# Weight sums, modulation rows, squares and the first w_mod of a two-layer denoising step: who does them, and when

## The chip, the cores and the metric

The kernel runs on one core of a Trainium2 chip. The metric is the device time of one execution in microseconds (us), from the profiler of the device; where several runs were made, their median.

## What is computed

A network of two layers works on 128 context tokens and 512 latent tokens, 640 in all (T), each 1024 numbers wide. In each layer, for the two groups of tokens:

```python
sh1, sc1, g1, sh2, sc2, g2 = split(silu(cond) @ w_mod + b_mod, 6)   # two conditions: context, latent
h = rmsnorm(x, norm1_g) * (1 + sc1) + sh1
z = h @ w_in                     # feeds an RG-LRU, two attentions and three branch gates
merged = sigmoid(ga) * (o_a @ w_oa) + sigmoid(gb) * (o_b @ w_ob) + sigmoid(gc) * (o_c @ w_oc)
x = x + g1 * (merged @ w_out)
h = rmsnorm(x, norm2_g) * (1 + sc2) + sh2
gate, val = split(h @ w_up, 2)   # 2 x 2816 columns
x = x + g2 * ((gelu(dwconv(gate)) * val) @ w_down)
```

After the layers a last RMSNorm gives the output. All is in 32-bit floating point.

## The kernel before

Tokens lie along the free dimension: an activation is eight tiles of 128 channels x 640 tokens. A matrix product in full precision is made of three (mm3): every operand is split into a high half (a rounded copy, made by ScalarE) and a low half (what is left, a subtraction on VectorE), and high x high, high x low and low x high are summed in PSUM. Tokens are worked in two halves of 320 columns.

**Order.** The program is a set of streams (generators): side (attention), lru, fill (modulation, `mod_stream`) and main. A clock that counts the estimated time of TensorE decides which stream goes on: a stream yields either a delay, or a mark of another stream (`("up", l)`, `("down", l, g)`, `("h", l, w, half)`) and a lag. TensorE's instructions stand in the order in which they are written. The other engines' instructions, and the DMA issues on SP, are put in order by a scheduler that goes by priority and by its own estimate of when an instruction is ready; `with self.soon(n)` makes instructions more urgent by n places, `MLOW = -200` less urgent. Each engine then works its list in order.

**Feed-forward part.** `ffn` makes the first three of 22 chunks of w_up directly (PLAIN). The other 19 are "pairs" (`pair`): a 2 x 2 block product done with seven smaller products instead of eight, in the order 1, 6, 7, 5, 4, 2, 3, each of 12 matmuls into one of six PSUM banks. `pair_weights` loads the four raw blocks of the next pair and makes their sums on GpSimd, in lines 1512 to 1515:

```python
e.tensor_tensor(out=s1, in0=a21, in1=a22, op=ALU.add)
e.tensor_tensor(out=a21, in0=a11, in1=a21, op=ALU.subtract)
e.tensor_tensor(out=s2, in0=s1, in1=a11, op=ALU.subtract)
e.tensor_tensor(out=s4, in0=a12, in1=s2, op=ALU.subtract)
```

`parts` makes the high (L1528) and low halves of a block after the current pair's product of the same number. For products 4, 2 and 3 (BY_DMA) the low half is made by ScalarE, which writes -x, and by a DMA with addition that GpSimd issues (L1531); for the others by VectorE (L1533). s1, s2 and s4 have one place each, used pair after pair. PSUM is read by VectorE (`add`, L1561). The gate's convolution is L1486 and L1488.

Chunks come in groups of 5, 4, 4, 4 and 5. After each group, `staggered` multiplies by the rows of w_down that belong to it (the down stage): eight output chunks, the first two together, each weight loaded and split by `wload` (L300 high, L303 low). `residual` scales by g2; in the first four groups (src is None) this is ScalarE's (L1363), and `done` adds the chunk to the tensor x_middle by a DMA with addition from GpSimd (L1691). In the last group, and in the output projection (`project`), `residual` also adds (VectorE, L1368), `square` sums the squares for the next RMSNorm (L608 on ScalarE, L610 on VectorE), and the last three chunks are worked half by half. After each half `norm_stream` forms the row sums of the squares on TensorE (`rstd`) and modulates the half (L657, L661, L662) with priority MSOON = 1500; the residual of these chunks has 3000.

**Modulation.** The vector of 6 x 1024 columns per layer is made in six parts v = 0 to 5 of eight blocks of 128 columns. `mods` makes parts by columns on TensorE: 32 matmuls of the condition (32 columns wide) with w_mod as the moving side into PSUM; the result is transposed. `mods_rows` makes one part on VectorE: for each block a load of 128 columns of the transposed w_mod (512 KB, tensor wmodt, L569), and two products with the condition that sum along the row (L578), with priority MLOW. The condition lies in four places of F (cond_rows, `get_cond`, L557). F is a pool of 22 places of 128 x 648 that all temporary tiles share; the place that has been free longest is given out.

In `mod_stream` layer 0's part 5 is made by columns after ("up", 0), layer 1's part 2 by rows after ("down", 0, 0) with a pace of 15, parts 0 and 1 by columns behind it, part 3 by rows after ("h", 1, 0, 1), part 4 by rows after the second attention, part 5 by columns after ("up", 1). At the very start parts 0 and 1 of layer 0 come from the tensor wmod in 32 loads of two runs of 1 KB a row (`start`, L1735).

Of the kernel before, what the change touches and what calls it, by code (L numbers as in the profile page):

```python
# [13 lines left out]
AF = mybir.ActivationFunctionType  # L14
ALU = mybir.AluOpType
AX = mybir.AxisListType

P = 128
D = 1024
KC = 8  # L20
SEQ = 128
LAT = 512
T = SEQ + LAT
# [5 lines left out]
FF_GROUPS = ((0, 5), (5, 4), (9, 4), (13, 4), (17, 5))  # L29
PLAIN = 3  # L30
# [142 lines left out]
class Net:  # L173
# [13 lines left out]
    MLOW, AFTER, PACE = -200, 8, (3.0, 2.0, 3.0, 15.0, 5.0)  # L187
# [6 lines left out]
    BY_DMA = (4, 2, 3)  # L194

# [287 lines left out]
    def mods(self, l, v, ahead=2, pace=0):  # L483

        n = 8 if v % 3 == 2 else 16
        yield from self.mods_columns(l, 8 * v, n, ahead, pace or self.PACE[1])
# [11 lines left out]
    def mods_columns(self, l, c0, n, ahead, pace):  # L498
# [16 lines left out]
        for k in range(KC):  # L515
            ws = q_.popleft()
            for j in range(4):
                o = j * w % 512
                self.matmul(
                    w / 2.2e3, out=acc[32 * j : 32 * j + 32, :w], lhsT=self.cond[:, k], rhs=ws[j * w // 512][:, o : o + w],  # L520
                    start=(k == 0), stop=(k == KC - 1), tile_position=(0, 32 * j),
                )
            self.F.put(*ws)
            if k + ahead < KC:
                q_.append(load(k + ahead))
            yield pace
# [830 lines left out]
    def residual(self, l, dst, src, b, m, half, gate):  # L1357
# [3 lines left out]
        for i, lo, hi in segs:  # L1361
            if src is None:
                self.nc.scalar.activation(  # L1363
                    out=dst[:, lo:hi], in_=b[:, lo - c0 : hi - c0], func=AF.Identity,
                    scale=self.mod[:, l, gate + m, i : i + 1],
                )
                continue
# [5 lines left out]
    def staggered(self, l, src, xs, gate, chunk, after, early, done=None, ahead=None, lead=None):  # L1373
# [20 lines left out]
        for m in range(n0, KC - late):  # L1394
            w = self.wload(src(m))
            x = chunk(m)
            for half in range(2):
# [24 lines left out]
        for half in range(2):  # L1422
            for w, x, m in zip(ws, cs, ms):
# [3 lines left out]
                if after is not None:  # L1427
                    self.square(x, m, half)
# [66 lines left out]
    @property  # L1495
    def sum_engine(self):
        return self.nc.gpsimd

    def pair_weights(self, l, j):


        nc, e = self.nc, self.sum_engine
# [11 lines left out]
        e.tensor_tensor(out=s2, in0=s1, in1=a11, op=ALU.subtract)  # L1514
        e.tensor_tensor(out=s4, in0=a12, in1=s2, op=ALU.subtract)
# [38 lines left out]
    def pair(self, l, j, ws, then, gv, during):  # L1554
# [44 lines left out]
        gv.append((xh, xl))  # L1599

# [6 lines left out]
    def ffn(self, l):  # L1607
# [28 lines left out]
        for g, (c0, nch) in enumerate(FF_GROUPS):  # L1636
# [60 lines left out]
            yield from self.staggered(l, src, gv, 40, chunk, after, early, done, ahead, lead)  # L1697
# [317 lines left out]
```

## Time and profile before

| | |
|---|---|
| median of 3 runs | 2439.75 us (2432.13 to 2444.91) |
| the profiled execution | 2437.27 us |
| its span, first to last instruction | 2435.5 us |
| TensorE busy | 2358.5 us, 97% |
| VectorE busy | 1721.6 us, 71% |
| ScalarE busy | 1189.1 us, 49% |
| GpSimd busy | 368.6 us, 15% |
| moved by DMA | 323.42 MB, 133 GB/s |

In the profile PE is TensorE, PEld its weight load, DVE VectorE, ACT ScalarE, POOL GpSimd, SP the queue that issues most DMAs. L578 is line 578 of the kernel. All times are of one execution; a matmul's end is modelled. PEclk is the granted clock of TensorE as a share of full speed (2.4 GHz).

### The profile page before, as it was taken

To read this page: it belongs to the slowest core of one execution; us is meant where nothing else is said; L and a number is where in the kernel's file an instruction comes from. 1 tells how busy PE (TensorE), PEld (TensorE's weight loads), DVE (VectorE), ACT (ScalarE), POOL (GpSimd) and SP (SyncE) were. 2 spreads that over 40 slices of the span, in tenths; PEclk is the share of its full clock that TensorE was granted. 3 is DMA by queue.
4 is the path that set the end of the run, shared out by engine and by line. 5 is a ranking of instruction groups with operands and counts; after the bars stand their busy time and mean duration, and the time that the engine had idled before them with its cause. 6 is when DMAs were issued, how large, how long until landed. Compare 5 with 4: busy or idle time off the path is not lost. (4 is left out here: it accounts for less than half of the span.)

```text
span 2435.5 us, 43194 instructions
## 1 busy us (share of the span) xinstructions
PE 2358.5 (97%) x16591; PEld 2254.8 (93%) x16591; DVE 1721.6 (71%) x3329; ACT 1189.1 (49%) x2413; POOL 368.6 (15%) x490
## 2 busy tenths in 40 slices
PE   8999999999999989999999999999999999999998
PEld 7899999998999888989999999999888989999998
DVE  6588878756767776655768688877667776755776
ACT  5237665723334445555543557565233354555553
POOL 0000000000000344444300000000000003543450
PEclk9999999999999999999999999999999999999999
DMA  8752222322552667685644322223226635656663
GB/s 289 236 180 72 91 71 82 98 66 72 158 177 85 187 160 177 169 209 118 173 158 146 100 91 79 82 71 97 64 76 203 207 118 125 152 126 148 136 147 115
DMA packets 162286, 323.42 MB, mean 133 GB/s; under 512 B 16272, under 2 KB 49568, under 8 KB 162080
## 3 DMA queue, kind: packets, MB, share of 16 engines
q1 hardware_dynamic: 140768, 277.66, 35.1%
q0 software_dynamic: 21312, 43.00, 11.1%
q8 instruction: 131, 2.15, 0.4%
q14 instruction: 75, 0.61, 0.1%
HBM read 244.29 MB, written 54.29 MB: 123 GB/s over the span
## 5 line engine op out<-in xcount | busy, mean ns | idle before, releaser
L277 PE MATMUL g<-r,wh 128*128 128x320 f32 (+1 forms) x5752 | 1304.7, 314 | 14.3 <-ACT f L1363 6.2
L277 PEld LDWEIGHTS g<-r,wh 128*128 128x128 f32 x5752 | 960.0, 189 | 43.3 <-issue 21.4
L277 PE MATMUL g<-r,wl 128*128 128x320 f32 (+1 forms) x2876 | 893.0, 311 | 13.8 <-DMA wl<-wr 4.8
L277 PEld LDWEIGHTS g<-r,wl 128*128 128x128 f32 x2876 | 544.3, 189 | 17.3 <-DMA wl<-wr 6.2
L303 DVE TENSOR_TENSOR wl<-wr,wh 128x1024 fp32r<-128x1024 f32 (+2 forms) x227 | 233.2, 1028 | 117.1 <-ACT wh L300 104.5
L277 PE MATMUL g<-r,k 128*128 128x320 f32 (+2 forms) x1256 | 216.4, 313 | 6.7 <-ACT f L1363 2.0
L277 PEld LDWEIGHTS g<-r,k 128*128 128x128 f32 x1256 | 192.4, 190 | 14.2 <-issue 3.3
L300 ACT CAST wh<-wr 128x512 fp32r<-128x512 f32 (+2 forms) x137 | 107.5, 785 | 168.9 <-PE g L277 98.7
L1470 POOL MEMSET f<- 128x1 f32 x132 | 31.9, 361 | 994.2 <-DMA f<-x_kept 226.8
L1001 DVE TENSOR_REDUCE sm<-s 128x1 f32<-128x640 f32 (+3 forms) x104 | 92.9, 893 | 89.1 <-PE s L277 88.6
L277 PE MATMUL g<-r 128*128 128x322 f32 (+2 forms) x628 | 124.1, 317 | 2.0 <-ACT f L1276 1.0
L1488 DVE SCALAR_TENSOR_TENSOR f<-f,vec 128x641 f32<-128x641 f32 x88 | 115.4, 1319 | 14.6 <-ACT f L1486 13.7
L277 PE MATMUL g<-wh,r 128*128 128x256 f32 x576 | 107.4, 282 | 0.0
L277 PEld LDWEIGHTS g<-r 128*128 128x128 f32 x628 | 100.5, 192 | 6.7 <-ACT f L1201 2.1
L578 DVE SCALAR_TENSOR_TENSOR s<-f 128x1024 f32<-128x1024 f32 x64 | 79.8, 1248 | 34.4 <-DMA f<-in_wmodt 28.9
L1528 ACT CAST wh<-f 128x512 fp32r<-128x512 f32 x116 | 71.0, 617 | 63.9 <-PE g L277 34.2
L277 PE MATMUL tb<-r,k 128*128 128x320 f32 x636 | 101.6, 309 | 0.3 <-DVE r L1586 0.3
L1363 ACT ACTIVATE f<-g,mod 128x192 f32<-128x192 f32 (+2 forms) x166 | 65.5, 436 | 70.5 <-PE g L277 55.5
L1533 DVE TENSOR_TENSOR wl<-f,wh 128x512 fp32r<-128x512 f32 x68 | 62.2, 920 | 51.8 <-ACT wh L1528 51.8
L1533 DVE TENSOR_TENSOR k<-f,k 128x512 fp32r<-128x512 f32 x78 | 63.8, 836 | 48.0 <-ACT k L1528 46.7
L1128 POOL MEMSET f<- 128x3 f32 (+1 forms) x48 | 4.3, 141 | 608.8 <-DMA q_kept<-f 151.3
L277 PEld LDWEIGHTS tb<-r,k 128*128 128x128 f32 x636 | 95.3, 188 | 0.5 <-DVE r L1586 0.5
(252 smaller groups left out, 4273.0 us busy)
## 6 DMA issues: line engine op xcount, KB each, us to landing
wr<-in_win SPq DMA_DIRECT2D x77, 512.0 KB, 3.4
f<-in_wmod SPq DMA_DIRECT2D x128, 256.0 KB, 4.5
wr<-in_wup SPq DMA_DIRECT2D x44, 512.0 KB, 4.7
f<-in_wup SPq DMA_DIRECT2D x40, 512.0 KB, 4.6
x_middle<-f POOLq DMA_DIRECT2D x64, 320.0 KB, 5.5
f<-in_wmodt SPq DMA_DIRECT2D x32, 512.0 KB, 4.7
wr<-in_wqkv SPq DMA_DIRECT2D x24, 512.0 KB, 4.0
wl<-f POOLq DMA_DIRECT2D x48, 256.0 KB, 5.2
```

The source lines that it names most:

```text
L277: self.nc.tensor.matmul(**kw)
L300: nc.scalar.copy(wh[:, :n], raw[:, :n])
L303: self.sub_engine().tensor_tensor(out=wl[:, o : o + c], in0=raw[:, o : o + c], in1=wh[:, o : o + c].bitcast(F32), op=ALU.subtract)
L578: nc.vector.scalar_tensor_tensor(out=junk, in0=w.ap, scalar=1.0, in1=self.cb[i].ap, op0=ALU.mult, op1=ALU.mult, accum_out=self.mod[:, l, j ...
L1001: nc.vector.tensor_reduce(out=m_[:, lo:hi], in_=src, axis=AX.XY if hi - lo == 1 else AX.X, op=ALU.max)
L1128: nc.gpsimd.memset(xp[:, c0:c1], 0.0)
L1363: self.nc.scalar.activation(out=dst[:, lo:hi], in_=b[:, lo - c0 : hi - c0], func=AF.Identity, scale=self.mod[:, l, gate + m, i : i + 1],)
L1470: nc.gpsimd.memset(gp[:, c : c + 1], 0.0)
L1488: nc.vector.scalar_tensor_tensor(out=g[:, :n], in0=gp[:, k : k + n], scalar=fw(k), in1=g[:, :n], op0=ALU.mult, op1=ALU.add)
L1528: self.nc.scalar.copy(h, x)
L1533: self.nc.vector.tensor_tensor(out=lo, in0=x, in1=h.bitcast(F32), op=ALU.subtract)
```

## The change

- `pair_weights`: the sums s2 and s4 are made by VectorE instead of GpSimd.
- `residual`, where it only scales: the second half is done by VectorE (tensor_scalar) instead of ScalarE.
- `staggered`, last chunks: `square` stands inside the same `soon(3000)` as the residual.
- `mod_stream`: layer 1's parts 0, 1 and 2 are all made by rows. Each step of `mods_rows` waits for the next mark of the list SLACK: the end of a pair that is not the last of its group, or the begin of output chunk 2, 3 or 4 of a down stage (29 marks, for 30 steps with 24 blocks). The condition is fetched once for the three. Parts 3 and 4 of layer 1 come one behind the other after ("h", 1, 0, 1), with a pace of 4.5 for 5.0.
- `mods_columns` does two of eight steps at a time (per = 2) with twice the pace, for part 5 of both layers.
- wmod is laid out in the order of its loads, one run of 2 KB a row.

The diff without its context lines:

```diff
@@ -187 +187 @@
-    MLOW, AFTER, PACE = -200, 8, (3.0, 2.0, 3.0, 15.0, 5.0)
+    MLOW, AFTER, PACE = -200, 8, (3.0, 2.0, 3.0, 0.0, 4.5)
@@ -195,0 +196,5 @@
+    SLACK = [
+        x for g, (c0, n) in enumerate(FF_GROUPS)
+        for x in [("pair", 0, j) for j in range(max(c0, PLAIN), c0 + n - 1)] + [("chunk", 0, g, m) for m in (2, 3, 4)]
+    ]
+
@@ -483 +488 @@
-    def mods(self, l, v, ahead=2, pace=0):
+    def mods(self, l, v, ahead=2, pace=0, per=1):
@@ -486 +491 @@
-        yield from self.mods_columns(l, 8 * v, n, ahead, pace or self.PACE[1])
+        yield from self.mods_columns(l, 8 * v, n, ahead, pace or self.PACE[1], per)
@@ -498 +503 @@
-    def mods_columns(self, l, c0, n, ahead, pace):
+    def mods_columns(self, l, c0, n, ahead, pace, per):
@@ -515,11 +520,12 @@
-        for k in range(KC):
-            ws = q_.popleft()
-            for j in range(4):
-                o = j * w % 512
-                self.matmul(
-                    w / 2.2e3, out=acc[32 * j : 32 * j + 32, :w], lhsT=self.cond[:, k], rhs=ws[j * w // 512][:, o : o + w],
-                    start=(k == 0), stop=(k == KC - 1), tile_position=(0, 32 * j),
-                )
-            self.F.put(*ws)
-            if k + ahead < KC:
-                q_.append(load(k + ahead))
+        for k0 in range(0, KC, per):
+            for k in range(k0, k0 + per):
+                ws = q_.popleft()
+                for j in range(4):
+                    o = j * w % 512
+                    self.matmul(
+                        w / 2.2e3, out=acc[32 * j : 32 * j + 32, :w], lhsT=self.cond[:, k], rhs=ws[j * w // 512][:, o : o + w],
+                        start=(k == 0), stop=(k == KC - 1), tile_position=(0, 32 * j),
+                    )
+                self.F.put(*ws)
+            for k in range(k0 + ahead, min(k0 + ahead + per, KC)):
+                q_.append(load(k))
@@ -1363,4 +1369,9 @@
-                self.nc.scalar.activation(
-                    out=dst[:, lo:hi], in_=b[:, lo - c0 : hi - c0], func=AF.Identity,
-                    scale=self.mod[:, l, gate + m, i : i + 1],
-                )
+                scale = self.mod[:, l, gate + m, i : i + 1]
+                if half:
+                    self.nc.vector.tensor_scalar(
+                        out=dst[:, lo:hi], in0=b[:, lo - c0 : hi - c0], scalar1=scale, scalar2=None, op0=ALU.mult
+                    )
+                else:
+                    self.nc.scalar.activation(
+                        out=dst[:, lo:hi], in_=b[:, lo - c0 : hi - c0], func=AF.Identity, scale=scale
+                    )
@@ -1373 +1384 @@
-    def staggered(self, l, src, xs, gate, chunk, after, early, done=None, ahead=None, lead=None):
+    def staggered(self, l, src, xs, gate, chunk, after, early, done=None, ahead=None, lead=None, name=None):
@@ -1396,0 +1408 @@
+            self.mark("chunk", l, name, m)
@@ -1427,2 +1439,2 @@
-                if after is not None:
-                    self.square(x, m, half)
+                    if after is not None:
+                        self.square(x, m, half)
@@ -1495,4 +1506,0 @@
-    @property
-    def sum_engine(self):
-        return self.nc.gpsimd
-
@@ -1502 +1510 @@
-        nc, e = self.nc, self.sum_engine
+        nc, e, v = self.nc, self.nc.gpsimd, self.nc.vector
@@ -1514,2 +1522,2 @@
-        e.tensor_tensor(out=s2, in0=s1, in1=a11, op=ALU.subtract)
-        e.tensor_tensor(out=s4, in0=a12, in1=s2, op=ALU.subtract)
+        v.tensor_tensor(out=s2, in0=s1, in1=a11, op=ALU.subtract)
+        v.tensor_tensor(out=s4, in0=a12, in1=s2, op=ALU.subtract)
@@ -1599,0 +1608 @@
+        self.mark("pair", l, j)
@@ -1697 +1706 @@
-            yield from self.staggered(l, src, gv, 40, chunk, after, early, done, ahead, lead)
+            yield from self.staggered(l, src, gv, 40, chunk, after, early, done, ahead, lead, g)
@@ -1727 +1735,0 @@
-        src = io["wmod"].rearrange("(r p) (g n c) -> n r p g c", p=P, g=2, n=n_)
@@ -1735 +1743 @@
-                nc.sync.dma_start(out=place.rearrange("p (g c) -> p g c", g=2)[:, :, :w], in_=src[n, r])
+                nc.sync.dma_start(out=place, in_=io["wmod"][n, r])
@@ -1883,2 +1891 @@
-        yield from self.mods(0, 5)
-        yield ("down", 0, 0), 0
+        yield from self.mods(0, 5, 2, 4.0, 2)
@@ -1886 +1893,4 @@
-        yield from self.mods_rows(1, 2, self.PACE[3], 1)
+        steps = deque(self.SLACK)
+        for v in range(3):
+            for x in self.mods_rows(1, v, 0, 1):
+                yield (steps.popleft(), self.PACE[3]) if steps else 0
@@ -1888,4 +1898,3 @@
-        yield from self.mods(1, 0, 2, 9.0)
-        for mark, v in ((("h", 1, 0, 1), 3), (("o", 1, 1), 4)):
-            yield mark, 0
-            self.get_cond()
+        yield ("h", 1, 0, 1), 0
+        self.get_cond()
+        for v in (3, 4):
@@ -1893,3 +1902,3 @@
-            self.F.put(*self.cb)
-        yield ("up", 1), 2
-        yield from self.mods(1, 5)
+        self.F.put(*self.cb)
+        yield ("up", 1), 0
+        yield from self.mods(1, 5, 2, 4.0, 2)
@@ -1910 +1919,3 @@
-    out = {"x": f(x.T.reshape(KC, P, T)), "wmod": f(i["w_mod"][0, :, : 2 * D])}
+    out = {"x": f(x.T.reshape(KC, P, T)), "wmod": i["w_mod"][0, :, : 2 * D]}
+
+    out["wmod"] = f(out["wmod"].reshape(KC, P, 2, 4, 256).transpose(3, 0, 1, 2, 4).reshape(4, KC, P, 512))
```

## Rows read from the trace of the kernel before

**Rows 1.** the page: busy us (share of the span) xinstructions
```profile
PE 2358.5 (97%) x16591; PEld 2254.8 (93%) x16591; DVE 1721.6 (71%) x3329; ACT 1189.1 (49%) x2413; POOL 368.6 (15%) x490
```

**Rows 2.** TensorE's waits, whole trace: us in total, times, longest us
```profile
PE g L277 <- ACT f L1363: 8.2, 8, 2.6
PE g L277 <- DVE wl L303: 6.7, 6, 3.6
PE pv L277 <- DMA wl<-wr: 6.5, 4, 2.5
PE pv L277 <- DVE f L610: 6.5, 2, 3.2
PE g L277 <- DMA wl<-wr: 4.8, 4, 1.9
PE g L277 <- DMA wl<-f: 4.1, 4, 1.7
```

**Rows 3.** windows after a wait: engines' busy us (xinstructions), then granted clock, DMA
```profile
756.70:763.60 6.90, 6.04 (x25) 6.05 (x26) 2.79 (x8) 0.17 (x1) 0.00 (x0) 0.51 0.22 76
```

**Rows 4.** windows: layer 0's and layer 1's feed-forward part
```profile
757.60:1244.30 486.70, 463.30 (x3084) 443.65 (x3084) 323.17 (x530) 246.40 (x484) 182.35 (x199) 0.98 0.64 164
1968.10:2424.60 456.50, 444.98 (x3018) 436.21 (x3018) 298.69 (x487) 241.26 (x475) 177.33 (x199) 0.99 0.56 133
```

**Rows 5.** timeline of VectorE, end of layer 0's output projection: start, us, engine, line
```profile
750.30 0.55 DVE L1368 SCALAR_TENSOR_TENSOR f<-g,mod,f 128x320 f32<-128x320 f32 x1 [0.19 <-PE g L277]
...
757.01 0.48 DVE L610 TENSOR_TENSOR f<-f 128x320 f32<-128x320 f32 x1
```

**Rows 6.** TensorE's groups by form: busy us, mean ns
```profile
L277 PE MATMUL s<-f,cond 128*32 128x512 f32 x128 | 17.0, 605 | 0.0
```

**Rows 7.** TensorE's waits between 1024 and 1056 us
```profile
PE g L277 <- ACT f L1363: 5.3, 4, 2.6
```

**Rows 8.** VectorE's groups by form: busy us, mean ns | idle before
```profile
L578 DVE SCALAR_TENSOR_TENSOR s<-f 128x1024 f32<-128x1024 f32 x64 | 79.8, 1248 | 34.4 <-DMA f<-in_wmodt 28.9 <-DMA f<-cond_rows 5.3
L1533 DVE TENSOR_TENSOR k<-f,k 128x512 fp32r<-128x512 f32 x78 | 63.8, 836 | 48.0 <-ACT k L1528 46.7 <-PE tb L277 1.2
...
L303 DVE TENSOR_TENSOR wl<-wr,wh 128x512 fp32r<-128x512 f32 x68 | 47.8, 702 | 65.8 <-ACT wh L300 65.2
...
L1368 DVE SCALAR_TENSOR_TENSOR f<-g,mod,f 128x320 f32<-128x320 f32 x24 | 13.1, 549 | 22.4 <-PE g L277 22.4
```

**Rows 9.** timeline of VectorE, layer 0's first down stage
```profile
853.47 1.23 DVE L578 SCALAR_TENSOR_TENSOR s<-f 128x1024 f32<-128x1024 f32 x1 [3.66 <-DMA f<-in_wmodt]
...
855.95 1.55 DVE L303 TENSOR_TENSOR wl<-wr,wh 128x640 fp32r<-128x640 f32 x2
```

**Rows 10.** windows at the begin of layer 1
```profile
1268.00:1318.50 50.50, 50.50 (x421) 50.50 (x420) 41.78 (x93) 15.08 (x31) 0.00 (x0) 1.00 0.48 157
1320.00:1360.00 40.00, 40.00 (x338) 40.00 (x338) 28.06 (x73) 11.38 (x28) 0.28 (x4) 1.00 0.50 155
```

**Rows 11.** TensorE's waits between 1795 and 1925 us
```profile
PE g L277 <- DVE r L1444: 2.6, 2, 1.4
```

**Rows 12.** GpSimd's groups by form: busy us, mean ns | idle before
```profile
L1514 POOL TENSOR_TENSOR f<-f 128x512 f32<-128x512 f32 x20 | 36.6, 1830 | 0.0
...
L1515 POOL TENSOR_TENSOR f<-f 128x512 f32<-128x512 f32 x20 | 27.7, 1384 | 73.1 <-DMA wl<-f 73.0
```

**Rows 13.** timeline of GpSimd, layer 0's second group
```profile
910.40 1.88 POOL L1514 TENSOR_TENSOR f<-f,wr 128x512 f32<-128x512 f32 x1
912.22 2.65 POOL L1531 DMA_DIRECT2D wl<-f  x3
```

**Rows 14.** timeline of TensorE at the same place
```profile
915.56 0.42 PE L277 MATMUL g<-r,wl 128*128 128x320 f32 x1 [1.69 <-DMA wl<-f]
```

**Rows 15.** window of the first loads of w_mod
```profile
12.70:19.90 7.20, 6.29 (x53) 5.39 (x53) 0.65 (x2) 0.88 (x3) 0.00 (x0) 0.73 1.08 388
```

**Rows 16.** GpSimd's waits, whole trace
```profile
POOL f L1515 <- DMA wl<-f: 104.7, 26, 5.2
```

## What I predict, and from what

> **What bounds the kernel now.** I read the page's busy times first. TensorE has work in 2358.5 us of a span of 2435.5 [rows 1], so 77 us of idle time are all that hiding something can win, besides work taken off TensorE itself. Then I read the list of what TensorE waits for [rows 2]: no wait is large. The reader is to see that four of its six rows belong to the feed-forward part (residuals on ScalarE, L1363; low weight halves that come by DMA, wl) and one, L610, to a single place in each layer. Next the windows after a wait [rows 3]: the granted clock is 0.51 of full, the lower level of 1.2 GHz, in a stretch that begins while TensorE stands still. The trace has three such stretches of 6.8 us after the first 23 us (from 756.7, 855.7 and 1968.4) and five of 3.4 us (from 900.1, 1186.8, 1261.9, 1866.0 and 1903.6). At half speed they lose 3.4 and 1.7 us each, about 19 us in all. A wait of 2 to 4 us can so cost twice its length. Last, the two feed-forward parts side by side [rows 4]: the same products take 486.7 us in layer 0 and 456.5 in layer 1, though TensorE's clock and instructions are alike. Layer 0's 30 us more are what the streams of modulation cost there: matmuls on TensorE, and waits.
>
> **The change part by part.** The sum is made against the profiled execution, 2437.3 us, which lies 2.5 below the median of the runs, 2439.75.
>
> *Squares first.* At the end of the output projection VectorE has the last residual done at 750.9, but the last sum of squares (L610) is run at 757.01, behind the first half's modulation, and TensorE waits until then for its row sums [rows 5]. That is 6.5 us in two waits [rows 2], each followed by a slow stretch of 6.8 us [rows 3], which costs 3.4. With the square as urgent as the residual (3000 against 1500 for modulation) it runs first and both go: 6.5 + 6.8 = 13.3. What it is put ahead of moves by one operation of 0.48 us, and TensorE reaches that half only after its 12 row sums. I take -13. At the end of layer 0 and of the kernel the same edit meets no wait of this size: 0.
>
> *Rows in place of columns for layer 1's first 16 columns.* Half of the 128 recorded matmuls in [rows 6] belong to mods(1, 0), and 17.0/2 = 8.5 us of TensorE work go: -8.5. Also gone are 32 loads of 256 KB on SP's queue; 16 of 512 KB come, the same bytes. The columns held eight places of F, the rows hold six (four for the condition, two for the load), but all through layer 0's feed-forward part. While the columns ran, residuals found no free place, since the last write to x_middle had not landed: 5.3 us of waits on L1363 [rows 7], of 8.2 in the whole trace [rows 2]. So some 3 us are spread over the other seven down stages. I leave 0.8 to this one: -4.5.
>
> *Where the row blocks stand.* One block is two products of 1.25 us [rows 8] on VectorE. Block 2 of layer 0's down stage shows the danger: the product stood 3.66 us before its load had landed, the low weights (L303) stood behind both products [rows 9], and TensorE waited 3.6 us, the longest wait on L303 [rows 2], and lost 3.4 more in the slow stretch from 855.7: -7 when these eight blocks are moved. But 24 blocks come, spread behind pairs and chunks. From one side they cost nothing: eight blocks ran between 1268 and 1318.5 with TensorE busy in 50.5 of 50.5 us [rows 10]. From the other, 7 us for those eight make 0.9 a block, 21 us. I take half, +11, since what decided was a load that came late, and the next load is still issued only one step ahead. Behind a chunk a step is short, so that end isn't excluded.
>
> *Modulation 4 moved from the second projection to behind modulation 3.* There VectorE's work delayed TensorE by 2.6 us on L1444 [rows 11] with two slow stretches of 3.4 (from 1866.0 and 1903.6): -2.6 - 3.4 = -6. In the new place VectorE is busy 28.06 of 40 us and TensorE without a gap [rows 10]: 0 there, at worst the 7 us of the eight blocks above.
>
> *Two of four weight sums to VectorE.* On GpSimd they are L1514 and L1515, 1.83 and 1.38 us [rows 12]. The low halves' DMAs are issued from the same queue: at 910.40 L1514 begins, at 912.22 the three DMAs follow [rows 13], TensorE waits for the first of them 1.69 us until 915.56 [rows 14]. Waits for such DMAs sum to 6.5 + 4.8 + 4.1 = 15.4 us in 12 [rows 2], 1.3 a wait, and two slow stretches (from 900.1 and 1186.8) add 3.4: 18.8. A DMA that is issued 1.8 us sooner closes most of them; one that stood behind L1512 or L1513, or before a landing that is late anyway, keeps its wait. Between 0 and -18.8 I take 60%: -11.
>
> *What VectorE gets for it.* 76 sums at 0.70 us (a subtraction of this size, L303) or 0.84 (the same while GpSimd works, L1533), and 64 residuals at 0.55, the price of L1368 with a PSUM operand [rows 8]. Layer 0's feed-forward part has 323 us of VectorE work in 487 [rows 4]; 38 sums (29), 32 residuals (18) and 16 blocks more (40) make 410 in about 465, 88%. Layer 1 comes to 299 + 29 + 18 = 346 of 446, 78%. VectorE at 41.78 of 50.5 us, 83%, did not stop TensorE [rows 10]; pairs are denser than that mean. Bounds: 0, and +15 if the excess over 83% in layer 0 (410 - 386 = 24 us) reaches TensorE in good part. I take +5. ScalarE loses the same residuals; it is no bound and I count nothing.
>
> *GpSimd's port, weighed.* The row for L1533 (0.84 against 0.70 for L303) says that a two-input operation runs slower while GpSimd adds [rows 8]; I use 0.84 only as the upper price. The Trainium skill, GPSIMD Engine Reference, Specifications, says that GpSimd shares its SBUF interfaces with VectorE and contends with instructions that have two SBUF inputs, as the moved sums have. By the page all 76 would be slowed, by the cheaper row none: some 10 us of VectorE time apart, which the bounds above hold.
>
> *First w_mod in loading order, two rows of columns at a time, pace.* While the first loads land, the DMA engines are full and move 388 GB/s [rows 15], so larger pieces can add little: even 5% of the 21.6 us that 8.4 MB take at this rate would be 1 us. I take 0. Eight column matmuls at a time in place of four are the same matmuls with as long a lead for their loads: 0.
>
> Sum: -13 - 8.5 - 4.5 - 7 + 11 - 6 - 11 + 5 = -34. 2437.3 - 34 = 2403; a median may lie a little above, as it does now: **2404 us**, 1.5% faster.
>
> **The rivals.**
>
> *VectorE becomes tight in layer 0.* Blocks cost 0.9 each (+21 for +11) and the added work +15 for +5: 2404 + 20 = 2424. For it: 88% on a mean, more in pairs. Against: blocks have the lowest priority and down stages leave VectorE half idle.
>
> *GpSimd's waits stay*, because the DMAs stand behind L1512 and L1513 or land late: 2404 + 11 = 2415. For it, the chain of two sums that is left; against, the 1.8 us read at 910.40.
>
> *The squares do not do what the change says.* If VectorE's order is not changed by the priority, 13 are not won: 2417. Little speaks for it; the residual beside it, with that priority, already ran ahead of modulation.
>
> *VectorE stands still for the last sum (slower).* L1515 overwrites a place that the previous pair's DMA still reads, and GpSimd waited 104.7 us in 26 waits for that landing [rows 16]. On GpSimd little stood behind it. On VectorE every PSUM reading and low half would; at 853.47 one late landing held L303 behind it [rows 9]. The point that decides is the share of this wait that reaches TensorE: a third (35 us) eats the whole gain, a half (52) gives 2404 - 5 + 52 = 2451. Against it: six banks of PSUM let TensorE run several products ahead, and the sum can be put later in the order than GpSimd had it. The Trainium skill says, in "DVE: scalar operands, raw-bit mode, write accounting and state across instructions", section 5, that VectorE's queue is one in-order queue; the trace agrees at 853.47, and this rival is what that rule makes of the change.
>
> *More than forecast*: all waits for low halves go and the blocks cost nothing: 2404 - 7.8 - 11 = 2385.
>
> **How the numbers follow.** Forecast 0.48 (its own range 2393 to 2412), more than forecast 0.10, GpSimd's waits stay 0.14, squares 0.07, VectorE tight 0.13, VectorE stands still 0.08. A measurement of this kernel tells about 0.5%, 12 us, from no change. Below 2427.5 lie the first four and two thirds of "tight": 0.86. From there to 2452 the rest of "tight" and half of "stands still": 0.08. Above: 0.06, with what I have not seen. The range takes in the better case and "tight" with its upper costs, 2382 to 2434; outside lie "stands still" and the tails.
>
> **What would show it.** Right: no wait on L610 and full clock after the output projections; no matmul of 512 columns on the condition after layer 0's start; L1514 and L1515 on VectorE, waits of TensorE for wl by DMA below 8 us; layer 0's feed-forward part some 465 us, layer 1's 446; no slow stretch near 1866 and 1904. Wrong: VectorE idle before L1515 on a DMA of wl or before L578 on its load, with TensorE waiting for L303, L1533 or L1561 just after; layer 0's feed-forward part still above 480 us.

## The result and the profile after

The changed kernel takes 2420.6 us (median of 5 runs, 2415.7 to 2422.3) against 2438.3 us for the kernel before beside it; the ratio is 0.9923, 95% interval 0.9898 to 0.9947. It is 0.8% faster: inside the range, but 17.8 us were won where 34 were forecast. Experiments below each carry a ratio to the kernel before that ran beside them. The interval of the changed kernel is 6 us to either side, those of the experiments 3 to 5, so a difference between an experiment and the changed kernel is known to some 7 to 8 us.

The page of the changed kernel, busy times (lines have moved: L578 is now L584, L303 L308, L1363 L1371 on VectorE and L1375 on ScalarE, L1368 L1379, L1514 and L1515 are L1522 and L1523):

```profile
PE 2345.7 (97%) x16523; PEld 2253.8 (93%) x16523; DVE 1785.0 (74%) x3532; ACT 1159.8 (48%) x2348; POOL 263.2 (11%) x414
```

TensorE has 12.8 us less to do than in [rows 1], GpSimd 105 less, VectorE only 63 more, and the span is 16.7 shorter. What TensorE waits for in the changed kernel, whole trace (us in total, times, longest):

```profile
PE g L282 <- DVE f L1371: 12.1, 5, 5.8
PE g L282 <- DVE wl L308: 6.4, 5, 4.1
PE g L282 <- ACT r L1593: 6.4, 4, 2.8
...
PE g L282 <- DMA wl<-wr: 2.4, 3, 1.6
```

Beside [rows 2]: the waits on sums of squares (6.5) are gone and those for low halves by DMA have fallen from 17.5 us in all (the rows shown there hold 15.4 of them) to 3.9; the residual of the second half, now VectorE's, has taken the first place with a longest wait of 5.8, and the end of a group's last pair (L1593) is new.

Where the time went is read from windows cut at the same events in both traces: the first row sums of squares after the output projection, the first matmul on the condition, the last row sums, and the first attention scores of layer 1. First the kernel before, then after; the columns are those of [rows 3] and [rows 4], so TensorE's idle time is the length less the first busy time.

```profile
741.00:791.50 50.50, 47.02 (x305) 45.99 (x304) 42.16 (x101) 28.77 (x59) 0.20 (x2) 0.93 0.27 93
791.50:1237.70 446.20, 424.42 (x2837) 405.72 (x2836) 290.12 (x460) 223.66 (x440) 182.15 (x197) 0.98 0.67 169
1237.70:1388.30 150.60, 145.88 (x1128) 143.82 (x1127) 113.66 (x264) 58.71 (x127) 0.61 (x8) 0.99 0.45 143
1388.30:1951.60 563.30, 554.68 (x3845) 524.64 (x3845) 421.90 (x826) 277.25 (x569) 3.08 (x26) 0.99 0.33 105
1951.60:2002.40 50.80, 47.30 (x307) 46.27 (x307) 42.20 (x101) 28.75 (x59) 0.00 (x0) 0.93 0.27 93
2002.40:2419.00 416.60, 406.48 (x2771) 398.48 (x2771) 267.12 (x419) 220.90 (x435) 177.33 (x199) 1.00 0.59 138
```

```profile
737.20:783.10 45.90, 44.42 (x308) 43.15 (x307) 42.26 (x101) 28.60 (x59) 0.00 (x0) 1.00 0.31 102
783.10:1231.20 448.10, 416.25 (x2767) 405.66 (x2767) 342.86 (x593) 209.00 (x407) 127.32 (x165) 0.98 0.66 167
1231.20:1387.20 156.00, 148.43 (x1129) 146.16 (x1127) 129.25 (x298) 57.62 (x127) 1.07 (x8) 0.97 0.52 168
1387.20:1941.10 553.90, 550.49 (x3844) 522.13 (x3845) 404.13 (x792) 278.05 (x569) 2.69 (x27) 1.00 0.30 97
1941.10:1985.20 44.10, 42.62 (x293) 41.38 (x291) 40.43 (x99) 27.49 (x58) 0.00 (x0) 1.00 0.31 105
1985.20:2401.70 416.50, 410.03 (x2783) 403.74 (x2783) 281.59 (x491) 207.65 (x405) 127.29 (x161) 0.99 0.59 138
```

The reader is to see three gains and two places where a gain was due and none came. After the output projections 4.6 and 6.7 us are won (1.8 of the 6.7 only because the first matmul on the condition, the cut, comes some 14 matmuls earlier: x293 against x307; with the squares alone, below, this stretch has x308 and takes 45.9), and the granted clock is 1.00 where it was 0.93. The 554 us of layer 1 up to its output projection are 9.4 shorter. But layer 1 begins 5.4 us slower, and the two feed-forward parts, from which 15 of the 34 us were to come (the terms for rows, sums and VectorE), keep their lengths: +1.9 and -0.1. In layer 0's part TensorE has 8.2 us less work and waits 31.9 us where it waited 21.8. Another 3.8 us lie ahead of the first cut (741.0 against 737.2); that is no gain of the change, since four kernels below that leave that stretch as before reach the cut at 737.8 to 738.7.

About half of what TensorE waits for in layer 0's part is one kind of chain, of which this is the longest case. SyncE, VectorE and TensorE in the changed kernel, in order of time (start, us, engine, line):

```profile
946.38 0.93 SPq L575 DMA_DIRECT2D f<-in_wmodt  x1
```

```profile
954.35 1.23 DVE L584 SCALAR_TENSOR_TENSOR s<-f 128x1024 f32<-128x1024 f32 x1 [7.00 <-DMA f<-in_wmodt]
...
956.83 0.55 DVE L1371 TENSOR_SCALAR f<-g,mod 128x320 f32<-128x320 f32 x1
...
957.89 0.55 DVE L1371 TENSOR_SCALAR f<-g,mod 128x320 f32<-128x320 f32 x1
```

```profile
958.49 1.97 PE L282 MATMUL g<-r,k 128*128 128x320 f32 x6 [5.83 <-DVE f L1371]
```

The load of a row block is issued when the block before it is done, at 946.38, and this one is also slow: it lands some 8 us later, where the median of these loads is 4.3. VectorE stands 7.0 us for it, two residuals run behind both products, and TensorE stands 5.8 us for the bank that the second of them empties. Layer 0's part has 39.2 us of such standing in 16 waits of VectorE (before: 17.9 in 7):

```profile
DVE s L584 <- DMA f<-in_wmodt: 39.2, 16, 7.0
```

Five of TensorE's waits of over 1 us come right behind such a stand, 16.2 of the 31.9 us; before it was one, of 3.6. My first theory was therefore that late loads cost the gain.

### The profile page after: what moved, and what is told of

It reads as the page before. It is cut to its first block, busy times and chain, and to the rows that moved or that the text cites. A ratio compares the mean times of both kernels' runs of the same rounds, so it can differ in the third digit from the quotient of the medians.

```text
span 2418.8 us, 43072 instructions
## 1 busy us (share of the span) xinstructions
PE 2345.7 (97%) x16523; PEld 2253.8 (93%) x16523; DVE 1785.0 (74%) x3532; ACT 1159.8 (48%) x2348; POOL 263.2 (11%) x414
## 4 chain that ended last, share of the span: by engine, by line
PE 70%; DVE 11%; DMA 9%; issue 5%; ACT 4%; POOL 1%; SPq 0%; DVEq 0%; POOLq 0%; ACTq 0%
PE g L282 52%; PE tb L282 5%; PE pv L282 5%; PE s L282 4%; DMA f<-in_wmodt 3%; PE tb L286 3%; DVE s L584 2%; DVE wl L308 1%; DMA wl<-f 1%; DMA f<-in_wup 1%; DVE f L1569 1%; DVE f L1500 1%; POOL f L1520 1%; DMA wr<-in_wup 1%; PE pv L286 1%
## 5 line engine op out<-in xcount | busy, mean ns | idle before, releaser
L308 DVE TENSOR_TENSOR wl<-wr,wh 128x1024 fp32r<-128x1024 f32 (+2 forms) x227 | 232.2, 1023 | 41.7 <-ACT wh L305 29.5
L305 ACT CAST wh<-wr 128x512 fp32r<-128x512 f32 (+2 forms) x137 | 107.0, 785 | 158.6 <-PE g L282 80.8
L584 DVE SCALAR_TENSOR_TENSOR s<-f 128x1024 f32<-128x1024 f32 x96 | 123.0, 1281 | 53.2 <-DMA f<-in_wmodt 52.7
L1482 POOL MEMSET f<- 128x1 f32 x132 | 15.4, 149 | 857.9 <-DVE r L776 360.7
L1500 DVE SCALAR_TENSOR_TENSOR f<-f,vec 128x641 f32<-128x641 f32 x88 | 92.2, 1055 | 3.2 <-ACT f L1498 2.4
L282 PE MATMUL s<-k,r 128*128 128x320 f32 (+3 forms) x448 | 92.4, 326 | 0.9 <-ACT k L903 0.9
L282 PEld LDWEIGHTS g<-wh,r 128*128 128x128 f32 x576 | 90.2, 188 | 3.4 <-issue 3.4
L1029 ACT ACTIVATE f<-s,sm,rs 128x640 f32<-128x640 f32 (+1 forms) x80 | 63.5, 796 | 62.0 <-DVE sm L1011 44.8
L775 ACT CAST r<-f 128x640 fp32r<-128x640 f32 (+2 forms) x72 | 51.5, 720 | 84.5 <-PE s L282 27.0
L1536 ACT CAST wh<-f 128x512 fp32r<-128x512 f32 x116 | 70.0, 614 | 42.5 <-PE g L282 22.8
```

The source lines that it names most:

```text
L282: self.nc.tensor.matmul(**kw)
L305: nc.scalar.copy(wh[:, :n], raw[:, :n])
L308: self.sub_engine().tensor_tensor(out=wl[:, o : o + c], in0=raw[:, o : o + c], in1=wh[:, o : o + c].bitcast(F32), op=ALU.subtract)
L584: nc.vector.scalar_tensor_tensor(out=junk, in0=w.ap, scalar=1.0, in1=self.cb[i].ap, op0=ALU.mult, op1=ALU.mult, accum_out=self.mod[:, l, j ...
L775: nc.scalar.copy(xh[:, :n], t[:, :n])
L1029: nc.scalar.activation(out=p[:, :n].rearrange("p (a c) -> p a c", a=2) if hi - lo == 1 else p[:, o : o + n], in_=src if hi - lo == 1 else ...
```

## Experiments

**Two loads ahead** (ratio 1.0021, 95% 1.0010 to 1.0033; 2442.9 us).

```
-            for x in self.mods_rows(1, v, 0, 1):
+            for x in self.mods_rows(1, v, 0, 2):
```

> The kernel after, but in layer 0's feed-forward part the load of a row block is issued two blocks ahead instead of one. Theory 1, VectorE stands at late row loads and the residuals of the second half stand behind it: VectorE's idle time before the row products on their load, 39.2 us in 16 waits after the change, falls below 10; TensorE's waits on the new VectorE residual fall from 11.4 to under 3 and those on the low weights (L308) from 5.5 to under 2; of the slow-clock stretches from 860, 925 and 955 two at least are gone; layer 0's feed-forward part, from the first matmul on the condition to layer 1's begin, takes 434 to 439 us instead of 448, and the kernel 2407 to 2412. Theory 2, VectorE simply has too much to do there: the waits for loads go as well, but TensorE's waits stay within 3 us of what they are, and the kernel stays at 2418 to 2422.

The kernel became 22 us slower than the changed one. Its window of layer 0's feed-forward part, then waits between 780 and 1260 us:

```profile
782.50:1251.50 469.00, 423.06 (x2767) 411.59 (x2767) 343.39 (x592) 207.82 (x407) 128.07 (x162) 0.96 0.63 160
```

```profile
PE g L282 <- ACT f L1375: 27.1, 14, 4.3
...
DVE f L1371 <- DMA x_middle<-f: 46.3, 13, 6.2
DVE s L584 <- DMA f<-in_wmodt: 13.0, 5, 7.0
...
ACT f L1375 <- DMA x_middle<-f: 60.7, 16, 8.2
```

Theory 1 was about right on the waits that it named: VectorE's on loads fell to 13.0 (below 10 was expected), TensorE's on L1371 to 0.8. It was wrong about the kernel. Residuals on both engines now wait 107 us for a write to x_middle to land (in the changed kernel 13.5), because the place in F that they write is still being read by it. The second load holds two more places. That can be the places or the second transfer; the next kernel tells them apart.

**Two places held and not used** (ratio 1.0070, 1.0053 to 1.0087; 2457.0 us).

```
         self.get_cond()
+        held = self.F.any_pair()
...
         self.F.put(*self.cb)
+        self.F.put(held)
```

> The kernel after, with two more places of F held through layer 0's feed-forward part and used for nothing; loads, products and their order are the same. It tells apart why two loads ahead made the kernel 22 us slower. Theory of places: F has too few, residuals find theirs only when the last write to x_middle has landed; then this kernel shows the same as two loads ahead: residuals wait for x_middle 60 to 110 us on ScalarE and VectorE together (13.5 on ScalarE after the change), layer 0's part takes 462 to 475 us instead of 448, and the kernel 2436 to 2446. Theory of transfers: a second load in flight delays the others; then the part keeps 446 to 452 us and the kernel 2418 to 2424.

```profile
785.30:1268.90 483.60, 428.90 (x2767) 415.35 (x2767) 344.71 (x593) 207.90 (x407) 129.81 (x161) 0.95 0.61 155
```

```profile
DVE f L1371 <- DMA x_middle<-f: 52.3, 14, 6.9
...
ACT f L1375 <- DMA x_middle<-f: 66.0, 18, 7.7
```

It is the places, and by more than I expected: two of them through layer 0's part cost 35.5 us there (483.6 against 448.1), with not one transfer more. Two loads ahead held as many places and had the part at 469.0: by that the earlier loads gave back 14.6. So a load ahead seems worth having; the room for it is not there.

**The residual back on ScalarE** (ratio 0.9968, 0.9952 to 0.9985; 2431.7 us).

```
-                if half:
+                if False:
                     self.nc.vector.tensor_scalar(
```

> The kernel after, with the residual of the second half back on ScalarE, the row loads as late as they were. Theory 1, what is behind the late product in VectorE's queue is what costs: TensorE's waits for that residual (11.4 us in layer 0) fall below 4, the waits on low weights (5.5) stay, VectorE stands at the row loads as long as before (39 us, within 6); the kernel 2408 to 2414. Theory 2, the residual is better on VectorE, and the waits come from the load on both engines: ScalarE's residuals wait as they did in the kernel before (8.2 us in all), and the kernel stays at 2417 to 2424.

Both theories fell: 11 us slower than the changed kernel. Waits between 780 and 1260 us:

```profile
PE g L282 <- DVE wl L308: 20.1, 7, 4.7
...
DVE s L584 <- DMA f<-in_wmodt: 48.5, 16, 5.8
...
DVE wl L308 <- ACT wh L305: 18.1, 9, 2.8
```

TensorE now waits for low halves (L308: 20.1 us; in the changed kernel 5.5). VectorE waits longer for the high halves of weights that ScalarE casts (L305: 18.1 us in 9; in the changed kernel 3.0 in 3), but that is not what TensorE's waits stand behind. Five of them, 18.4 us together, come right after a stand of VectorE of 4.3 to 5.8 us at a row load, with the low half behind the product. The longest stand:

```profile
857.91 1.23 DVE L584 SCALAR_TENSOR_TENSOR s<-f 128x1024 f32<-128x1024 f32 x1 [5.81 <-DMA f<-in_wmodt]
...
860.39 0.82 DVE L308 TENSOR_TENSOR wl<-wr,wh 128x640 fp32r<-128x640 f32 x1
```

The cast of this half had ended at 855.3, and TensorE had waited 4.1 us by 861.3. So it is the late load again, with low halves behind it where the changed kernel has mostly residuals. That the row products stand ahead of the low halves here because the casts come behind residuals fits VectorE's longer waits for casts, but no run shows it. The move was worth 11 us in the changed kernel; on the kernel before, or without the rows, it was not run.

**Rows alone, on the kernel before** (ratio 1.0092, 1.0071 to 1.0113; 2461.3 us). The new stream with its marks, without the rest:

```
-        yield ("down", 0, 0), 0
         self.get_cond()
-        yield from self.mods_rows(1, 2, self.PACE[3], 1)
+        steps = deque(self.SLACK)
+        for v in range(3):
+            for x in self.mods_rows(1, v, 0, 1):
+                yield (steps.popleft(), 0.0) if steps else 0
         self.F.put(*self.cb)
-        yield from self.mods(1, 0, 2, 9.0)
```

> The kernel before with one edit, layer 1's first three modulations by rows behind pairs and chunks, no columns for the first two. The forecast's terms: 8.5 us of TensorE work, 4.5 of waits and 7 of the old eight blocks go, 24 blocks bring 11: 9 us faster, 2429. Theory of late loads: the row loads, one block ahead, hold up VectorE's low weights as in the kernel after (some 30 us of idle time before the products on their load), but the residuals are on ScalarE and do not stand behind them, so TensorE loses 5 to 8 us: 2423 to 2431, and layer 0's feed-forward part takes 432 to 440 us instead of 446. Rival, the blocks cost what the columns cost wherever the residuals are: 2436 to 2442, and the part takes 445 to 450.

```profile
789.50:1254.90 465.40, 423.92 (x2769) 411.05 (x2768) 322.83 (x523) 222.68 (x439) 183.58 (x203) 0.97 0.64 161
```

All three were far too low. TensorE is idle for 41.5 us of this part where it was idle for 21.8, at a lower mean clock. VectorE stands 51.4 us at row loads (before: 17.9), and TensorE's waits right behind such stands sum to 12.5 us in five (before: 3.6 in one). Its waits for low halves by DMA rise too, to 15.6 us from 9.5; why, the runs do not settle. Rows in place of columns make the kernel before 23 us slower.

**Columns kept, in the changed kernel** (ratio 0.9876, 0.9859 to 0.9893; 2408.5 us). The lines of the experiment above, the other way round.

> The kernel after, with layer 1's first two modulations by columns on TensorE again and the third by rows behind layer 0's first down stage, as before the change; the rest as after. Theory 1, the rows' 24 blocks cost more than the 8 to 12 us of TensorE work that they save, because they stand in VectorE's queue on late loads and hold six places of F through the whole part: VectorE's idle time on row loads falls from 39 us to under 20, layer 0's feed-forward part takes 428 to 440 us instead of 448, and the kernel 2402 to 2413. Theory 2, with residuals and sums on VectorE the rows are worth their place: the part takes 447 to 456 us and the kernel 2420 to 2429.

```profile
783.40:1223.00 439.60, 422.85 (x2836) 405.43 (x2836) 302.81 (x530) 208.65 (x408) 127.06 (x158) 0.98 0.68 172
```

Three of the waits there:

```profile
ACT f L1375 <- DMA x_middle<-f: 33.5, 8, 10.2
DVE s L584 <- DMA f<-in_wmodt: 17.7, 6, 7.3
DVE f L1371 <- DMA x_middle<-f: 14.6, 3, 5.8
```

Theory 1 holds: 8.5 us less in this part than after, 12 in the kernel. The columns' work is back (TensorE busy 422.9 for 416.3), but TensorE is idle for 16.8 us in place of 31.9. Its waits right behind a stand at a row load are 5.2 us in two, where they were 16.2 in five: 11 of the 15 us. The places do not explain the difference: residuals wait more for a write to x_middle here (48.1 us) than in the changed kernel (13.5). By these waits the places are what stops a second load, not what the single load costs. In both surroundings the rows lose.

**The two weight sums alone, on the kernel before** (ratio 0.9972, 0.9959 to 0.9986; 2431.7 us).

```
-        e.tensor_tensor(out=s2, in0=s1, in1=a11, op=ALU.subtract)
-        e.tensor_tensor(out=s4, in0=a12, in1=s2, op=ALU.subtract)
+        v.tensor_tensor(out=s2, in0=s1, in1=a11, op=ALU.subtract)
+        v.tensor_tensor(out=s4, in0=a12, in1=s2, op=ALU.subtract)
```

> The kernel before with one edit, two of four weight sums on VectorE. The forecast's term: TensorE's waits for low weights by DMA (15.4 us in both layers) fall to some 6, with the slow stretches behind them 11 us, less up to 5 for VectorE's added work: 2427 to 2433. Theory of the trace after: in layer 1 the third sum on VectorE earns 7 to 9 us and the last gives 7 back, so layer 1's part keeps 415 to 419; layer 0's part gains from neither by more than 4: 442 to 450; the kernel 2434 to 2440.

Its two feed-forward parts:

```profile
789.40:1239.60 450.20, 425.75 (x2837) 406.25 (x2836) 290.09 (x498) 222.62 (x440) 125.92 (x159) 0.98 0.67 168
...
2004.80:2417.90 413.10, 405.66 (x2771) 398.56 (x2771) 265.55 (x457) 220.36 (x435) 127.10 (x161) 1.00 0.59 139
```

Layer 0 gains nothing (kernels that leave these parts as before have 446.2 to 450.1 there and 416.6 to 419.3 in layer 1), layer 1's trace is 3.5 to 6.2 us shorter, and the kernel gains 6.8 by its ratio. TensorE's waits for low halves by DMA do fall, from 17.5 us in all to 6.4.

**The last sum on GpSimd** (ratio 0.9939, 0.9920 to 0.9959; 2423.3 us), and **in layer 1 alone** (0.9889, 0.9873 to 0.9905; 2411.6 us).

```
-        v.tensor_tensor(out=s4, in0=a12, in1=s2, op=ALU.subtract)
+        e.tensor_tensor(out=s4, in0=a12, in1=s2, op=ALU.subtract)            # both layers
+        (e if l else v).tensor_tensor(out=s4, in0=a12, in1=s2, op=ALU.subtract)   # layer 1
```

> The kernel after, with the last of the four weight sums (s4) back on GpSimd and the third (s2) on VectorE. Theory 1, the forecast's rival, VectorE stands still for the place that the last sum overwrites and its adds stand behind: the 23 us of VectorE's idle time before that sum are gone, the waits of TensorE at a group's last pair on the gated halves (about 3.5 us in layer 1 from 2.5 and 1.0) shrink to under 2, and the kernel is 2 to 5 us faster, 2416 to 2419. Theory 2, the last sum on GpSimd holds up the DMAs of low halves queued behind it: GpSimd waits some 100 us for the place, TensorE's waits for low weights by DMA rise from under 3 to 6 to 10 us, and the kernel is 3 to 10 us slower, 2424 to 2431.

> The kernel after, with the last weight sum (s4) on GpSimd in layer 1 alone. When it was on GpSimd in both layers, layer 1's feed-forward part (from the first matmul on the condition to the last row sums) took 409.7 us instead of 416.5, layer 0's 459.4 instead of 448.1. If each layer's change comes from its own sum, this kernel has 448 in layer 0 and 410 in layer 1, and takes 2412 to 2415. Rival: layer 0's difference is only how the products, loads and waits fall, and no cost of the sum; then layer 0 may land anywhere from 445 to 462, and the kernel from 2410 to 2427.

The feed-forward parts of the first, then of the second:

```profile
783.90:1243.30 459.40, 422.97 (x2769) 413.92 (x2768) 341.80 (x574) 210.02 (x407) 156.34 (x184) 0.96 0.64 163
...
1995.00:2404.70 409.70, 406.05 (x2782) 400.63 (x2782) 282.64 (x472) 207.20 (x405) 153.71 (x180) 1.00 0.60 141
```

```profile
783.30:1229.80 446.50, 417.78 (x2768) 407.73 (x2768) 341.81 (x593) 209.04 (x407) 128.29 (x165) 0.97 0.66 168
...
1982.10:2391.70 409.60, 405.99 (x2784) 400.69 (x2783) 278.88 (x472) 207.90 (x405) 154.37 (x180) 1.00 0.60 141
```

Neither theory fitted the first kernel as a whole: layer 1 becomes 6.8 us shorter, layer 0 11.3 longer. The second shows that each layer's change is its own sum's. In layer 1 the last sum on VectorE costs: VectorE stands for the place that this sum overwrites (14.2 us in 13 waits in the changed kernel's layer 1), an add of a product's bank stands behind it, and the gated halves of a group's last pair come late (TensorE's waits on L1593 and L1594 there sum to 5.4 us, and to 0.5 in the second kernel). Without it TensorE's idle time there is 3.6 us instead of 6.5, and the clock 1.00. In layer 0 the same sum on GpSimd has TensorE wait more for L308 and for a low half by DMA (10.1 and 5.0 us); why it does so in this layer only, the runs do not settle.

**Squares alone** (0.9966, 0.9953 to 0.9980; 2430.7 us) and **modulation 4 alone** (0.9981, 0.9965 to 0.9998; 2434.0 us), on the kernel before.

```
-                if after is not None:
-                    self.square(x, m, half)
+                    if after is not None:
+                        self.square(x, m, half)
```

> The kernel before with one edit, the last squares and their sums as urgent as the residual. The forecast's step: the two waits on the sum of squares (6.5 us) and the two slow-clock stretches from 756.7 and 1968.4 (3.4 each) go, 13.3 us, and the kernel takes 2424 to 2427. Rival, from the trace after: only the two stretches from the row sums to the first matmul on the condition are 4.6 and 6.7 us shorter, 11.3, but layer 1 begins 5.4 us later, because modulation is put behind the squares at the end of layer 0 too; then this kernel shows the same longer begin of layer 1 (156 us instead of 151) and takes 2430 to 2433.

```
-        for mark, v in ((("h", 1, 0, 1), 3), (("o", 1, 1), 4)):
-            yield mark, 0
-            self.get_cond()
+        yield ("h", 1, 0, 1), 0
+        self.get_cond()
+        for v in (3, 4):
             yield from self.mods_rows(1, v, self.PACE[4], 1)
-            self.F.put(*self.cb)
+        self.F.put(*self.cb)
```

> The kernel before with one edit, modulation 4 of layer 1 right behind modulation 3. The forecast's step: the slow-clock stretches from 1866 and 1903.6 and the 2.6 us of waits on L1444 go, 6 us, and the kernel takes 2430 to 2434. Rival, the whole stretch from layer 1's first matmuls to its output projection is 9.4 us shorter after the change by this edit: 2428 to 2430. If neither, that stretch keeps its 563 us and the gain there came from something else.

Squares, the two stretches after the output projections; then modulation 4, layer 1's begin and the stretch behind it:

```profile
737.80:783.80 46.00, 44.51 (x309) 43.25 (x310) 42.26 (x101) 28.60 (x59) 0.20 (x2) 1.00 0.31 102
...
1947.50:1993.40 45.90, 44.41 (x308) 43.15 (x308) 42.26 (x101) 28.56 (x59) 0.00 (x0) 1.00 0.31 103
```

```profile
1236.10:1391.30 155.20, 147.82 (x1129) 145.30 (x1127) 129.52 (x298) 58.16 (x127) 1.07 (x8) 0.98 0.53 166
1391.30:1945.10 553.80, 550.41 (x3843) 522.12 (x3844) 404.05 (x792) 277.86 (x569) 2.68 (x27) 1.00 0.31 97
```

The squares win 4.5 and 4.9 us there, both slow stretches are gone, and layer 1's begin is not longer (151.9). Modulation 4 wins 9.5 us where it left and gives 4.6 back where it went, in layer 1's begin: idle time 7.4 us for 4.7.

**First w_mod in loading order alone** (0.9996, 0.9981 to 1.0012; 2440.1 us).

```
-                nc.sync.dma_start(out=place.rearrange("p (g c) -> p g c", g=2)[:, :, :w], in_=src[n, r])
+                nc.sync.dma_start(out=place, in_=io["wmod"][n, r])
...
```

> The kernel before with one edit, the first w_mod in loading order. The forecast's term: 0, 2438 within 2. Rival, read from the trace after: the stretch up to the first scores is 3.0 us shorter for this edit, so it shows here as 184.4 instead of 187.4, and the kernel is 2 to 4 us faster.

No difference that can be told (4.6 us faster to 2.9 slower). The first scores come at 186.0 us; with the old layout they come at 184.4 to 187.4 in the traces of this study, so the 3.0 us that I had read off two traces are their scatter.

**Both that helped together**: columns kept, and the last sum on GpSimd in layer 1 alone (ratio 0.9843, 0.9824 to 0.9862; 2401.3 us).

> The kernel after with both edits that were faster alone: layer 1's first two modulations by columns again, and the last weight sum on GpSimd in layer 1 alone. If they add up, layer 0's feed-forward part takes 440 us, layer 1's 409 to 410, and the kernel 2403 to 2407, under both. If layer 1's part gains nothing beyond the columns' kernel (412.6 there), it stays at 2407 to 2410.

```profile
785.30:1227.30 442.00, 421.05 (x2835) 403.95 (x2835) 303.04 (x529) 209.13 (x408) 126.98 (x158) 0.99 0.68 171
...
1979.10:2387.10 408.00, 404.74 (x2782) 400.53 (x2782) 277.93 (x472) 208.06 (x405) 154.10 (x180) 1.00 0.60 141
```

They add up, within the spread (2403 to 2407 was expected). It is the fastest version here, 0.8% under the changed kernel.

## Why the prediction held, and which terms did not

The time lies in the range, but outside the forecast's own 2393 to 2412, and that it lies in the range is in part luck: one step had the wrong sign, and a saving that had been counted as nothing made up for about what that step cost. The signs of being wrong that the prediction named came too: layer 0's feed-forward part above 480 us, and VectorE idle before the row products with TensorE waiting just after.

*Squares, -13.* Right in mechanism, too large: 9.4 us in the two stretches, 8 by the ratio. The two L610 waits went and the clock stayed up, but TensorE then waits 1.2 us in each for what comes next (0.6 each on L632 and L662), so that 4.0 us of waiting went and not 6.5. I had counted the stall as gone and had not said what is late behind it. The clock gave back 5.4 us (busy 47.0 and 47.3 before, 44.5 and 44.4 with the squares alone), not 6.8.

*Rows for columns and where the blocks stand: -8.5 - 4.5 - 7 + 11 = -9.* The step that failed. The work that leaves TensorE was sized right (8.2 us less after; half of [rows 6] is left). The rest was not: rows alone made the kernel 23 us slower, and in the changed kernel they cost 12. The term that was far too small is what the blocks cost, +11. The next block's load is issued only when a block is done: I named it, and took 0.45 us a block between 0 and 0.9. If the other three terms, 20 us, are left as they stand, the 24 blocks cost 43 us on the kernel before, 1.8 each, and 32 in the changed kernel, 1.3 each. What the traces show in place of 0.45 is a queue that stands: VectorE's 39.2 us at row loads, with residuals and low halves behind them. The -7 did not come either: at 859.0 TensorE waits 4.1 us behind a late block, as it had waited 3.6 at 856.8. The -4.5 for the places did come in the changed kernel: TensorE waits 5.7 us on ScalarE's residuals with columns kept and not at all after. But the six are held all through, two more cost 35.5 us, and I had not asked how near the pool was to its end. The upper bound came from eight blocks with another queue around them, and it was no bound.

*Modulation 4, -6.* -4.6 by its ratio (interval -0.5 to -8.5), about as forecast, out of two sizes that were both off: 9.5 won where it left (6 forecast), 4.6 lost where it went (0 forecast, 7 at worst).

*Sums to VectorE, -11, and what VectorE gets, +5.* The waits for low halves fell by 11 us in the kernel with this edit alone, as was forecast for waits and clock together; the kernel gained 6.8, near the sum of the two terms; the gain that its traces show lies in layer 1. The prices were right: in the changed kernel's groups by form, L1522 takes 0.80 us and L1523 0.69 or, in its other form, 0.85 (forecast 0.70 to 0.84), the residual 0.55.

```profile
L1371 DVE TENSOR_SCALAR f<-g,mod 128x320 f32<-128x320 f32 x54 | 29.7, 550 | 78.4 <-PE g L282 78.4
L1522 DVE TENSOR_TENSOR f<-f 128x512 f32<-128x512 f32 x20 | 16.0, 800 | 14.6 <-POOL f L1520 14.3 <-DMA f<-in_wup 0.3
...
L1523 DVE TENSOR_TENSOR f<-f 128x512 f32<-128x512 f32 x20 | 13.8, 688 | 19.2 <-DMA wl<-f 19.2
```

*ScalarE "is no bound and I count nothing".* Wrong by 11 us in the changed kernel (4 to 18 by the intervals). ScalarE is 49% busy in [rows 1], yet taking residuals from it changed what stands behind the late row products. Why the order of VectorE's queue changes with it is argued, not shown. This saving hid about what the rows cost.

*First w_mod, 0.* Right. The other changes counted as 0, two steps of columns at a time and the pace, were not run alone.

*The sum.* -8 for the squares, +12 for the rows, -5 for modulation 4, -7 for the sums and -11 for the residuals make -19, what the ratio of the changed kernel gives. Each is uncertain by 3 to 7 us, and with the 23 us of rows alone it would be -8: the pieces do not simply add.

*The rivals.* By its time, 2424, "VectorE becomes tight in layer 0" came nearest, and by its place: the feed-forward part of layer 0, by the cuts of [rows 4] 751.2 to 1238.8, takes 487.6 us where I expected 465, layer 1's (1955.1 to 2407.3) 452 for 446. But VectorE is not full: 343 of 448 us. Its added work gained time, and it is its order that costs. "GpSimd's waits stay" did not come (17.5 us fell to 3.9), nor did the rival on the squares. "VectorE stands still for the last sum" is real in layer 1, at 7 us and not 52: it stood 23 us in 19 waits for that place, not GpSimd's 104.7 [rows 16]. The Trainium skill, "DVE: scalar operands, raw-bit mode, write accounting and state across instructions", section 5, has VectorE's queue in order; the stand at 954.35 with the residual behind it is that rule at work. I had counted with such a stand for low halves behind a row product [rows 9] and for the last sum, not for the residuals that the change puts into the same queue.

## What to carry to other kernels

Before work is spread over a whole stage, count the buffers that it holds there and find who waits for one: here two places of F cost 35 us while every transfer and product stayed the same. A low share of busy time does not make an engine free: ask what stands behind an instruction that itself waits. Low-priority work that waits for a transfer is not low priority once it is at the head of an in-order queue.

## What had not been expected of the hardware

How much of a loss is not waiting but slower matmuls. Three kernels have the same 2767 matmuls in layer 0's feed-forward part. TensorE is idle there for 31.9, 45.9 and 54.7 us (after, two loads ahead, places held), the mean granted clock is 0.98, 0.96 and 0.95, and the same matmuls are busy for 416.3, 423.1 and 428.9 us. So of the 35.5 us that two places cost, 22.8 are waiting and 12.7 are matmuls at a lower clock. The prediction had this for single waits, not for a stage.

GpSimd's additions slow single operations of VectorE. In layer 0's part of the kernel before, operations of VectorE with two inputs of 128x512 that its timeline lists singly took 0.68 to 0.69 us where no addition of GpSimd ran beside them (79), and 1.4 on the mean where one ran for more than half of their time (21); at 905.32, beside L1515, a low half (L1533) took 1.45. In the changed kernel 17 such operations took 1.15 on the mean, more than half of them no longer than alone.

Two traces of kernels that are alike in a stretch differ there by up to 4 us (446.2 to 450.1 in layer 0's part), and by 6 in layer 1's, which columns kept, after, places held and two loads ahead share (412.6, 416.5, 417.5 and 418.6); of the two traces alone, the start and the beginning of layer 1 could not have been read.
